# TensorE's queue written out by hand from the late features to the end of attention

## The chip, the cores and the metric

The kernel runs on one core of one Trainium2 chip. A time is the device time of one execution in microseconds (us). Three executions of the kernel before took 1167.98, 1169.8 and 1173.2 us; their median, 1169.8, is the time before. The names of the engines in the profile are PE (TensorE matmul), PEld (TensorE weight load), DVE (VectorE), ACT (ScalarE), POOL (GpSimd) and SP (SyncE, which issues most DMAs).

## The reference

One layer of a decoder on 1024 positions of width 1024, in float32. Three groups of heads read the same normed input, and one output projection mixes them. A gated MLP follows.

```python
h = rms_norm(x, norm1_g)
proj = h @ w_in            # q 512 | k 512 | v 512 | forget gates 8 | conv a 256, b 256 | pool 256
q, k = rms_norm per head of 64;  att = forgetting_attention(q, k, v, fg + b_f)
conv = conformer_conv(conv_in, ...)      # a*sigmoid(b), 31 causal taps, LayerNorm, silu, @ conv_pw
pool = multiscale_pool(pool_in, ...)     # means over 2/4/8/16 positions minus self, @ pool_w, scale
x = x + concat([att, conv, pool]) @ w_out
up = causal_depthwise_conv(rms_norm(x, norm2_g) @ w_up, ffn_dw_w)
x = x + (silu(gate) * val) @ w_down

# forgetting_attention, for a block of 128 queries and the keys up to its end (8 heads of 64):
s = q @ k.T * 64**-0.5 + cum[query] - cum[key]     # cum: running sum of log_sigmoid(fg)
p = softmax(where(key <= query, s, -1e30)); out = p @ v
```

## The kernel before

Every matmul is made of three: each operand is split into a rounded high half and a low half (`split`: ScalarE casts the high half, L48; VectorE, or GpSimd where it is named, subtracts for the low half, L49), and `mm3` adds high x high (L53), high x low (L54) and low x high (L55). A sum stays in one PSUM bank of 128 x 512 floats until an engine evacuates it.

The stages, in the program's order:

- Features. The convolution's a and b and the pool input are projected. The first two blocks go with the arriving weights; the others (the late features, from L341) follow one after the other, in the banks named `mm`, of which there are four.
- Values (`values_in`). Eight tiles of 128 positions, eight k each: first 256 columns (192 matmuls), then 256 columns and the 8 gate logits. ScalarE evacuates each tile into `v` (L424) and `fgt` (L426).
- The gates (`gate_cumsum`). VectorE and ScalarE turn the logits into log gates `fz` (L368 to L375), TensorE transposes them (L381), and their running sum goes to DRAM as `cumd`, from where each head's row comes back as `ck`.
- Q and K (`heads_in`). Q in tiles of 512 columns, two tiles at a time with k outside, then K in two calls of 256 columns. Each tile is squared (ScalarE), reduced (VectorE), turned into a scale (GpSimd), and scaled into `qk` (VectorE, L460), which frees the bank. The weights of Q's last four k are split in turn by VectorE and GpSimd, into `w` out of the raw buffers `wr`.
- Work at the side (`side_work`, a generator that is stepped between the tiles): 31 taps for each of two channel blocks and two halves of the positions (`taps`, VectorE, L268, 120 multiply-adds of 128 x 512 and 4 starts), the pool's running means and differences `d` with their split `dhl` and product (`pool_work`, products into the banks named `tp`, two of them), and the convolution's LayerNorm, silu and product (`conv_tail`: transposes, `s_` with its split, products, all in `tp` banks).
- `prep_pair`. For two heads, Q and K are transposed (L402) and split into `qT`, `kh`, `kl`, four pieces of four transposes per pair.
- Attention. A stage is one head and one group g of two query blocks, in the order g = 3, 0, 2, 1. `scores` issues the products (L534, with the causal mask added as a product, L537), VectorE adds the running gate and keeps the row minimum in one pass (L539), ScalarE takes the exponential (L543), VectorE the reciprocal of the sum (L545), GpSimd scales (L546). `values` transposes the probabilities `p` into a bank `t`, up to four blocks of 128 at a time (L558), splits the bank into `pt`, and multiplies with the head's `vhl` (L567 to L569); the output goes to `matt` (L574). Scores run three stages ahead (`LOOK`). Between stages, the parts of the output projection that need only convolution and pool (`mix_out`, banks `f`) and the next heads' `prep_pair` are put in.
- Behind it the attention part of the output projection (banks `c`), the MLP's up and down projections.

What sets the order: the queue of each engine is written by the framework's scheduler, which simulates the program and issues what it finds ready, by the program's order where several are. So the generators and the places of `step` are hints, and TensorE's queue interleaves single matmuls of different parts. Each engine then runs its queue strictly in order; a waiting instruction holds what stands behind it. An order written by hand (`tc.manual_schedule`) exists in before only for SP in the last stage.

## Time and profile before

| | |
|---|---|
| median of three runs | 1169.8 us |
| the profiled execution | 1172.92 us, its span 1170.7 us |
| TensorE / VectorE / ScalarE / GpSimd busy | 1099.4 / 896.1 / 534.4 / 342.3 us |
| late features end | 79.4 us |
| first score product, last value product | 254.4 us, 442.9 us |
| up projection | about 512 to 926 us |

A busy TensorE is a union of matmul intervals with modelled ends; what it works through is better read from the distance of starts. The profile's rows by window have, for each engine, its busy time and the number of instructions, then the granted TensorE clock (1.00 is full speed). Rows of a timeline begin with start and duration. Rows of groups have "count | busy time, mean ns of one | idle time ahead of them and its releaser". An arrow `a <- b` in the names reads: a is written from b.

### The profile page before, as it was taken

The page shows a single profiled execution, that of the slowest core. Times are in us where ns is not written, and L with a number is a line of the kernel's source. Part 1 is how long each engine was busy: PE and PEld are TensorE (multiplying, and loading weights), DVE is VectorE, ACT ScalarE, POOL GpSimd, SP SyncE. Part 2 cuts the span into 40 slices and gives each one's busy share as a digit, 9 for nine tenths or more (in the row PEclk, how much of TensorE's full clock was granted, in tenths as well). Part 3 has the DMA queues.
Part 4 walks back from the last instruction along what each step waited for, and adds up shares of the span by engine and source line. Part 5 has one row for each costly group of instructions (what it writes and reads, how often), then busy time and mean ns, then how long its engine had stood idle before and what let it go on. Part 6 is the DMA issues. An engine that isn't in the chain of part 4 may idle for free.

```text
span 1170.7 us, 14708 instructions
## 1 busy us (share of the span) xinstructions
PE 1099.4 (94%) x5476; PEld 912.8 (78%) x5476; DVE 896.1 (77%) x1262; ACT 534.4 (46%) x785; POOL 342.3 (29%) x335
## 2 busy tenths in 40 slices
PE   7995998899999989869999999999999999899987
PEld 6775977887888878758888888888888787688865
DVE  5899996468888665777887878788887655898673
ACT  7331322358878754445353535353544443243321
POOL 1480447557667742301212121212121210000010
PEclk9997999999999989969999999999999999899999
DMA  9130111033124131211212221212121497672362
GB/s 353 37 98 15 37 38 54 2 109 101 53 81 127 36 127 73 108 37 55 92 70 79 84 100 63 100 63 93 70 102 60 136 330 261 215 261 91 126 224 82
DMA packets 52792, 124.15 MB, mean 106 GB/s; under 512 B 6249, under 2 KB 11753, under 8 KB 49905
## 3 DMA queue, kind: packets, MB, share of 16 engines
q1 hardware_dynamic: 47056, 103.29, 26.4%
q0 software_dynamic: 5664, 19.93, 4.3%
q8 instruction: 43, 0.70, 0.2%
q14 instruction: 29, 0.23, 0.1%
HBM read 99.04 MB, written 19.96 MB: 102 GB/s over the span
## 4 chain that ended last, share of the span: by engine, by line
PE 58%; DVE 16%; issue 15%; DMA 5%; ACT 2%; POOL 2%; SPq 1%; POOLq 0%; DVEq 0%; ACTq 0%
PE b L55 12%; PE b L53 12%; PE b L54 12%; DVE acc L268 8%; PE s L534 2%; PE t L558 2%; DMA xr<-in_xT_dram 1%; PE f L53 1%; PE mm L53 1%; PE mm L54 1%; PE f L55 1%; PE c L53 1%; PE mm L55 1%; PE px L567 1%; PE f L54 1%
## 5 line engine op out<-in xcount | busy, mean ns | idle before, releaser
L865 POOL TENSOR_TENSOR ac<-ac 128x1024 f32<-128x1024 f32 x22 | 61.4, 2792 | 368.5 <-ACT u L846 266.5
L821 DVE SCALAR_TENSOR_TENSOR ac<-u,par,ac 128x1023 f32<-128x1023 f32 x88 | 112.6, 1280 | 8.9 <-ACT ac L819 7.9
L268 DVE SCALAR_TENSOR_TENSOR acc<-u,par,acc 128x512 f32<-128x512 f32 x120 | 105.9, 935 | 0.0
L53 PE MATMUL mm<-w,hh 128*128 128x256 f32 (+2 forms) x320 | 99.0, 311 | 3.8 <-DVE qk L460 3.8
L48 ACT CAST wsh<-ws 128x2048 fp32r<-128x2048 f32 x22 | 42.0, 1910 | 130.0 <-PE b L54 129.8
L54 PE MATMUL mm<-w,hh 128*128 128x256 f32 (+2 forms) x320 | 98.8, 310 | 0.0
L55 PE MATMUL mm<-w,hl 128*128 128x256 f32 (+2 forms) x320 | 98.8, 309 | 0.0
L49 DVE TENSOR_TENSOR dl<-dr,dh 128x1024 fp32r<-128x1024 f32 (+1 forms) x39 | 65.7, 1684 | 26.9 <-ACT dh L48 26.9
L546 POOL TENSOR_TENSOR p<-p,l 128x896 f32<-128x896 f32 (+3 forms) x64 | 72.7, 1150 | 32.0 <-DVE l L545 30.5
L48 ACT CAST dh<-dr 128x1024 fp32r<-128x1024 f32 (+1 forms) x39 | 54.6, 1401 | 58.5 <-PE y L55 24.6
L54 PE MATMUL x<-dl,dh 128*128 128x512 f32 x176 | 70.2, 399 | 4.8 <-DVE dl L49 4.8
L915 POOL DMA_DIRECT2D out_dram<-acc x16 | 8.7, 541 | 211.1 <-DVE acc L911 210.5
L55 PE MATMUL x<-dh,dl 128*128 128x512 f32 x176 | 69.8, 396 | 0.0
L53 PEld LDWEIGHTS mm<-w,hh 128*128 128x128 f32 x320 | 61.9, 193 | 7.4 <-issue 4.2
L819 ACT ACTIVATE ac<-u,par 128x1024 f32<-128x1024 f32 x44 | 50.7, 1152 | 31.2 <-DVE u L856 30.7
L54 PEld LDWEIGHTS mm<-w,hh 128*128 128x128 f32 x320 | 62.1, 194 | 3.3
L55 PEld LDWEIGHTS mm<-w,hl 128*128 128x128 f32 x320 | 62.2, 194 | 3.1
L48 ACT CAST dh<-res 128x1024 fp32r<-128x1024 f32 x22 | 23.1, 1052 | 87.6 <-PE y L55 63.4
L53 PE MATMUL x<-dh 128*128 128x512 f32 x176 | 54.9, 406 | 6.3 <-DVE acc L911 5.6
L49 DVE TENSOR_TENSOR wsl<-ws,wsh 128x2048 fp32r<-128x2048 f32 x22 | 50.4, 2290 | 12.8 <-ACT wsh L48 12.8
L49 DVE TENSOR_TENSOR pt<-t,pt 128x512 fp32r<-128x512 f32 (+1 forms) x80 | 49.5, 631 | 12.5 <-ACT pt L48 12.2
L714 DVE TENSOR_TENSOR ws<-wur 128x512 f32<-128x512 f32 x21 | 58.4, 2783 | 0.0
(316 smaller groups left out, 3327.3 us busy)
## 6 DMA issues: line engine op xcount, KB each, us to landing
wur<-in_w_up_dram SPq DMA_DIRECT2D x22, 1024.0 KB, 4.9
dr<-in_w_down_dram SPq DMA_DIRECT2D x66, 256.0 KB, 5.0
dr<-gd SPq DMA_DIRECT2D x55, 256.0 KB, 4.6
gd<-ac POOLq DMA_DIRECT2D x22, 512.0 KB, 3.0
wr<-in_w_in_dram SPq DMA_DIRECT2D x32, 256.0 KB, 2.7
res<-gd SPq DMA_DIRECT2D x22, 256.0 KB, 5.6
v<-in_x_dram SPq DMA_DIRECT2D x8, 512.0 KB, 8.9
ck<-cumd SPq DMA_DIRECT2D x8, 512.0 KB, 3.6
```

Source lines behind the costliest of these rows:

```text
L48: nc.scalar.copy(out=dst_hi, in_=src)
L49: (lo or nc.vector).tensor_tensor(out=dst_lo, in0=src, in1=dst_hi.bitcast(F32), op=ALU.subtract)
L53: nc.tensor.matmul(ps, a_hi, b_hi, start=first, stop=False, skip_group_check=more)
L54: nc.tensor.matmul(ps, a_hi, b_lo, start=False, stop=False, skip_group_check=more)
L55: nc.tensor.matmul(ps, a_lo, b_hi, start=False, stop=last, skip_group_check=more)
L268: nc.vector.scalar_tensor_tensor(out=a, in0=u[:, c, o + j:o + j + 512], scalar=pc(PC_DW + c * CW + j), in1=a, op0=ALU.mult, op1=ALU.add)
L534: nc.tensor.matmul(ps[:, 0:c1 - c0], qT[:, i * P:(i + 1) * P], part[:, c0:c1], start=b == 0, stop=b == 1 and c1 < n)
L546: nc.gpsimd.tensor_tensor(out=pt[:, 0:n], in0=pt[:, 0:n], in1=l[:, 1:2].broadcast_to([P, n]), op=ALU.mult)
L714: eng.tensor_tensor(out=out, in0=a, in1=b, op=ALU.subtract)
L819: nc.scalar.activation(out=ac, in_=us, func=AF.Copy, scale=pc(w0 + 2))
L821: nc.vector.scalar_tensor_tensor(out=ac[:, j:S], in0=us[:, 0:S - j], scalar=pc(w0 + 2 - j), in1=ac[:, j:S], op0=ALU.mult, op1=ALU.add)
L865: nc.gpsimd.tensor_tensor(out=a[:, 1], in0=a[:, 1], in1=a[:, 0], op=ALU.mult)
```

## The change

From the late features to the end of attention TensorE's queue is now the program's order (`manual_schedule` for PE). The other engines are still ordered by the scheduler, which simulates them against that queue. The program's order is rewritten with it:

- The work at the side is parted. VectorE's own work (`vector_work`: taps and pool sums, from which `d`) is still stepped between tiles; what TensorE takes part in (`side_work`: the pool product, now `pool_out`, and `conv_tail`) is put at fixed groups of Q's and K's matmuls: the gate transposes behind Q's k=6, pieces of `side_work` behind every second k from 9 on, in K behind every fifth, and the first `prep_pair` inside K's second call.
- `log_gates` is cut off from `gate_cumsum` and issued after the values.
- The raw weight buffer `wr` is half as wide; the pool `rp` has four buffers instead of three.
- Attention is 80 turns of one bank of transposes. In a round k: transposes of turn k, scores (12 steps per 10 turns, 10 steps ahead), a `prep_pair` piece in three windows of rounds (2 to 8, 22 to 28, 42 to 48, every second), a quarter of a `mix_out` tile (rounds 10 to 49 four times in five, from 52 in each, two at times), then the value products of turn k-2 (`LAG`).
- The banks `t` go from three to two, the banks `px` from one to two, `ms` from one buffer to two, and `ms` with its rows of x is prepared a tile ahead (`mix_prep`). `load_cum` is moved out of `prep_head`, two heads ahead. Of the value products of a turn, the low half for j0 now comes last.

The diff, cut to its core:

```diff
-    rp = pa2.enter_context(tc.tile_pool(name="rp", bufs=3, **right))
+    rp = pa2.enter_context(tc.tile_pool(name="rp", bufs=4, **right))
...
-            t = rp.tile([P, 1056], F32, name=name, bufs=2)
+            t = rp.tile([P, 528], F32, name=name, bufs=2)
...
+    def pool_out(i):
+        hl_ = []
+        for half in range(2):
+            dhl = sp.tile([P, 2, 512], F32R, name="dhl", tag="shl")
+            split(dhl[:, 0], dhl[:, 1], pool_d[i][:, half * 512:half * 512 + 512])
+            hl_.append(dhl)
+        yield
+        for half in range(2):
+            ps = tpps()
+            mm3(ps, pw_hl[:, 0, i, :], pw_hl[:, 1, i, :], hl_[half][:, 0], hl_[half][:, 1], True, True)
+            nc.vector.tensor_scalar(out=mcp[half][:, 2 + i, :], in0=ps, scalar1=pc(PC_PS + i), scalar2=None,
+                                    op0=ALU.mult)
+            yield
...
+    def vector_work():
+        yield from taps(0)
+        pool_consts()
+        yield from pool_sums(0)
+        yield from pool_sums(1)
+        yield from taps(1)
+
     def side_work():
-        yield from taps(0)
-        yield from pool_work()
-        yield from taps(1)
+        yield from pool_out(0)
+        yield from pool_out(1)
         yield from conv_tail(0)
         yield from conv_tail(1)
 
-    bg = side_work()
+    vw, sw = vector_work(), side_work()
...
+    ordered = ExitStack()
+    ordered.enter_context(tc.manual_schedule(engines={mybir.EngineType.PE}))
...
-            step(7)
+            step(6)
...
+                side(t0 // per * KT + k)
...
+    values_in(C_V, 256, 0, later(load_two, 4, C_V + 256, 264, nc.gpsimd), 2)
+    values_in(C_V + 256, 264, 1, later(load_wide, 4, 0, nc.gpsimd), 2)
     for k in range(4, KT):
         load_wide(0, k, (nc.vector, nc.gpsimd)[k % 2])
-    gate_cumsum()
-    heads_in(0, 0, 512, later(load_two, 4, 512, 256, None), 6)
-    for _ in bg:
+    log_gates()
+
+    def side_q(n):
+        step(1 if n < 19 else 9)
+        if n == 6:
+            gate_cumsum()
+        elif n >= 8 and n % 2:
+            next(sw, None)
+
+    heads_in(0, 0, 512, later(load_two, 4, 512, 256, None), side_q)
+    heads_in(512, 1, 256, later(load_two, 4, 768, 256, nc.gpsimd), lambda n: n % 5 == 4 and next(sw, None))
...
+    heads_in(768, 1, 256, [], lambda n: n in (4, 12, 20, 28) and next(pp, None))
...
-    psT = pb.enter_context(tc.tile_pool(name="psT", bufs=3, space=PSUM))
-    psX = pb.enter_context(tc.tile_pool(name="psX", bufs=1, space=PSUM))
+    psT = pb.enter_context(tc.tile_pool(name="psT", bufs=2, space=PSUM))
+    psX = pb.enter_context(tc.tile_pool(name="psX", bufs=2, space=PSUM))
...
+    def turn(h, g, jj):
         p0, p1 = pr_t[h, 2 * g], pr_t[h, 2 * g + 1]
-        po = xbank()
-        for jj in range(g + 1):
-            ps = psT.tile([P, 512], F32, name="t", tag="t")
-            j0, j1 = 2 * jj, 2 * jj + 1
-            srcs = [(p0, j0), (p1, j0), (p1, j1)] if jj == g else [(p0, j0), (p1, j0), (p0, j1), (p1, j1)]
-            for a, (p, j) in enumerate(srcs):
-                nc.tensor.transpose(out=ps[:, a * P:(a + 1) * P], in_=p[:, j * P:(j + 1) * P], identity=ident)
-            n = len(srcs) * P
-            pt = bp.tile([P, 2, 512], F32R, name="pt", bufs=4)
-            split(pt[:, 0, 0:n], pt[:, 1, 0:n], ps[:, 0:n])
-            c = 512 - n if jj == g else 0
-            for b in range(2):
-                if jj == 0 and b == 1:
-                    pt0 = pt
-                else:
-                    nc.tensor.matmul(po[:, 0:256], vhl[:, j0, :], pt[:, b, 0:256], start=jj + b == 0, stop=False)
-                nc.tensor.matmul(po[:, c:256], vhl[:, j1, :], pt[:, b, 256:n], start=False, stop=False)
-        nc.tensor.matmul(po[:, 0:256], vhl[:, 0, :], pt0[:, 1, 0:256], start=False, stop=True)
+        ps = psT.tile([P, 512], F32, name="t", tag="t")
+        j0, j1 = 2 * jj, 2 * jj + 1
+        srcs = [(p0, j0), (p1, j0), (p1, j1)] if jj == g else [(p0, j0), (p1, j0), (p0, j1), (p1, j1)]
+        for a, (p, j) in enumerate(srcs):
+            nc.tensor.transpose(out=ps[:, a * P:(a + 1) * P], in_=p[:, j * P:(j + 1) * P], identity=ident)
+        n = len(srcs) * P
+        pt = bp.tile([P, 2, 512], F32R, name="pt", bufs=4)
+        split(pt[:, 0, 0:n], pt[:, 1, 0:n], ps[:, 0:n])
+        return pt, n
+
+    def values(h, g, jj, pt, n, po):
+        vhl = hd[h]
+        c = 512 - n if jj == g else 0
+        j0, j1 = 2 * jj, 2 * jj + 1
+        nc.tensor.matmul(po[:, 0:256], vhl[:, j0, :], pt[:, 0, 0:256], start=jj == 0, stop=False)
+        for b in range(2):
+            nc.tensor.matmul(po[:, c:256], vhl[:, j1, :], pt[:, b, 256:n], start=False, stop=False)
+        nc.tensor.matmul(po[:, 0:256], vhl[:, j0, :], pt[:, 1, 0:256], start=False, stop=jj == g)
...
+            for n in range(4):
+                w = wo[4 + n, half]
+                mm3(ps, m[:, 0, n, :], m[:, 1, n, :], w[:, 0], w[:, 1], n == 0, n == 3)
+                if n == 1 and t % 4 < 3:
+                    nxt = mix_prep(t + 1, half)
+                if n == 3:
+                    nc.vector.tensor_tensor(out=x2_slice(t, half), in0=ps, in1=xr, op=ALU.add)
+                yield
...
+    stages = [(h, g) for h in range(H) for g in (3, 0, 2, 1)]
+    turns = [(n, jj) for n, (h, g) in enumerate(stages) for jj in range(g + 1)]
+
+    def all_scores():
+        for n, st in enumerate(stages):
+            for _ in scores(*st):
+                yield n
...
+    LAG = 2
+    sc = all_scores()
+    done = [sum(g + 1 for h, g in stages[:n]) for n in range(len(stages) + 1)]
     prep_head(0)
-    for st in stages[:LOOK]:
-        scores(*st)
-    pp = None
-    for n, (h, g) in enumerate(stages):
-        at = n // 4
-        if n % 4 == 0 and at + 1 < H:
-            prep_head(at + 1)
-        if n + LOOK < len(stages):
-            scores(*stages[n + LOOK])
-        if n % 8 == 1 and at + 2 < H:
-            pp = prep_pair(at // 2 + 1, fbank)
-        if pp is not None:
-            next(pp, None)
-            prep_done[0] |= at == 5 and n % 8 == 7
-        values(h, g)
-        if n >= 4 and (n % 2 == 0 or n > 28):
-            next(fill, None)
-    for _ in fill:
-        pass
+    load_cum(1, bp)
+    n_sc, last = 0, 0
+
+    def more_scores(upto, turned):
+        nonlocal n_sc, last
+        while n_sc < upto and last is not None:
+            nxt = n_sc // 12 * 4 + (0, 0, 0, 0, 1, 1, 2, 2, 2, 2, 3, 3)[n_sc % 12]
+            if nxt >= 4 and turned < done[nxt - 3]:
+                break
+            last = next(sc, None)
+            n_sc += 1
+
+    more_scores(10, 0)
+    pairs = {k: pr for pr, k0 in ((1, 2), (2, 22), (3, 42)) for k in range(k0, k0 + 8, 2)}
+    preps = {}
+    fill1, fill2 = mix_first(), mix_second()
+    banks, waiting = {}, []
+
+    def value(n, jj, pt, w):
+        h, g = stages[n]
+        if jj == 0:
+            banks[n] = xbank()
+        values(h, g, jj, pt, w, banks[n])
+
+    for k, (n, jj) in enumerate(turns):
+        h, g = stages[n]
+        if k % 10 == 2 and h + 1 < H:
+            prep_head(h + 1)
+        if k % 10 == 3 and h + 2 < H:
+            load_cum(h + 2, bp)
+        waiting.append((n, jj, *turn(h, g, jj)))
+        more_scores(10 + (12 * (k + 1)) // 10, k + 1)
+        if k in pairs:
+            if pairs[k] not in preps:
+                preps[pairs[k]] = prep_pair(pairs[k], fbank)
+            next(preps[pairs[k]])
+        if k >= 10 and k < 50:
+            run(fill1, (k % 5 != 0))
+        if k >= 52:
+            run(fill2, 1 + (k % 8 == 0))
+        if len(waiting) > LAG:
+            value(*waiting.pop(0))
+    run(fill1, 32)
+    while waiting:
+        value(*waiting.pop(0))
+        run(fill2)
+    run(fill2, 32)
```

How the queues move, at three places. The first is ScalarE's queue during the first values: `v_134` are evacuations of the first values' tiles, `dhl` the high halves of the pool difference. Before:

```order
L48 CAST w<-wr 128x2x264 x2
L424 ACTIVATE v_134<-mm,rstd 128x256 x5
L48 CAST dhl<-d 128x512 x2
L424 ACTIVATE v_134<-mm,rstd 128x256 x2
L48 CAST w<-wr 128x512 x2
```

With the change:

```order
L48 CAST w<-wr 128x2x264 x2
L446 ACTIVATE v_134<-mm,rstd 128x256 x4
L48 CAST dhl<-d 128x512 x2
L446 ACTIVATE v_134<-mm,rstd 128x256 x3
L48 CAST w<-wr 128x512 x2
```

The casts of `dhl` have moved ahead of the fifth evacuation.

The second is TensorE's queue around the gate transposes, during Q (`hh_118` is the eighth part of the normed input that belongs to k=4, and so on; 79 of Q's 192 matmuls stand ahead of the transposes). Before:

```order
L53 MATMUL mm<-w,hh_118 128x512
L54 MATMUL mm<-w,hh_118 128x512
L55 MATMUL mm<-w,hl_126 128x512
L53 MATMUL mm<-w,hh_119 128x512
L381 MATMUL tp<-ident,fz 8x128 x8
L54 MATMUL mm<-w,hh_119 128x512
L55 MATMUL mm<-w,hl_127 128x512
```

With the change:

```order
L53 MATMUL mm<-w,hh_120 128x512
L54 MATMUL mm<-w,hh_120 128x512
L55 MATMUL mm<-w,hl_128 128x512
L403 MATMUL tp<-ident,fz 8x128 x8
L53 MATMUL mm<-w,hh_121 128x512
L54 MATMUL mm<-w,hh_121 128x512
L55 MATMUL mm<-w,hl_129 128x512
```

Now 42 of Q's matmuls stand ahead of them, those of k=0 to k=6 of the first two tiles.

The third is TensorE's queue in attention: `t` transposes, `s` scores, `px` value products, `f` the fill. Before, near the start:

```order
L568 MATMUL px<-pt,vhl 128x256
L558 MATMUL t<-ident,p_2506 128x128
L534 MATMUL s<-kh,qT 128x512
L534 MATMUL s<-kl,qT 128x512
L567 MATMUL px<-pt,vhl 128x256
L568 MATMUL px<-pt,vhl 128x128
L558 MATMUL t<-ident,p_2521 128x128
L558 MATMUL t<-ident,p_2506 128x128
```

With the change, one round in the second half:

```order
L585 MATMUL t<-ident,p_4371 128x128
L585 MATMUL t<-ident,p_4403 128x128
L561 MATMUL s<-kh,qT 128x128
L561 MATMUL s<-kl,qT 128x128
L564 LDWEIGHTS ident_b
L564 MATMUL s<-mask_b,ident_b 128x128
L53 MATMUL f<-wo,ms 128x512
L54 MATMUL f<-wo,ms 128x512
L55 MATMUL f<-wo,ms 128x512
L595 MATMUL px<-pt,vhl 128x256
L597 MATMUL px<-pt,vhl 128x256 x2
L598 MATMUL px<-pt,vhl 128x256
```

Single transposes and products were interleaved; now transposes, scores, fill and value products of a round each stand together.

More of the change, by code (lines that the diff above doesn't have):

```diff
@@ L299, in conv_tail @@
             yield
+        yield
         for n in range(2):
@@ L430, in values_in, with heads_in @@
                     m()
-    def heads_in(c0, src, w, then, steps):
+    def heads_in(c0, src, w, then, side):
         chunks = range(2) if w == 512 else (c0 // 256 % 2,)
@@ L523, in scores @@
         qT, kh, kl = qkT[h]
-        vhl, ck = hd[h]
+        ck = cks[h]
         for i in (2 * g, 2 * g + 1):
@@ new lines, in scores @@
+                if c1 == n:
+                    l = bp.tile([P, 2], F32, name="l", bufs=8)
+                    nc.scalar.activation(out=pt[:, 0:n], in_=pt[:, 0:n], func=AF.Exp, scale=-1.0, bias=init,
+                                         accum_out=l[:, 0:1])
+                    nc.vector.reciprocal(out=l[:, 1:2], in_=l[:, 0:1])
+                    nc.gpsimd.tensor_tensor(out=pt[:, 0:n], in0=pt[:, 0:n], in1=l[:, 1:2].broadcast_to([P, n]),
+                                            op=ALU.mult)
+                    pr_t[h, i] = pt
@@ L621, in mix_work, with mix_second @@
         yield from mix_out(1, 0)
-        while not prep_done[0]:
-            yield
+    def mix_second():
         load_wo(1, 4, bp)
@@ L652, in tile_hybrid_block, with run @@
-    for _ in fill:
-        pass
+    def run(it, n=1):
+        for _ in range(n):
+            next(it, None)
+    LAG = 2
+    sc = all_scores()
+    done = [sum(g + 1 for h, g in stages[:n]) for n in range(len(stages) + 1)]
+    prep_head(0)
+    load_cum(1, bp)
[8 more added lines that the diff above has]
+            n_sc += 1
```

114 lines of the change are left out of this document (46 added, 68 removed).

## The prediction

> **What bounds the kernel now.** I read the page first, then the busy time of each engine stage by stage, then TensorE's waits, then single rows.
>
> ```profile
> span 1170.7 us, 14708 instructions
> PE 1099.4 (94%) x5476; PEld 912.8 (78%) x5476; DVE 896.1 (77%) x1262; ACT 534.4 (46%) x785; POOL 342.3 (29%) x335
> ```
>
> TensorE is busy for 94% of the span. An order can only win the rest, stretches at half clock, and the gaps that modelled ends hide. The stages that the change reorders lie between 79.4 (late features done) and 443.2 us (last value product):
>
> ```profile
> core 0: us, PE busy (x) PEld busy (x) DVE busy (x) ACT busy (x) POOL busy (x), PEclk, DMA share, GB/s
> 79.40:159.10 79.70, 66.59 (x464) 62.83 (x463) 79.63 (x111) 21.05 (x45) 22.78 (x11) 0.91 0.15 41
> 159.10:254.40 95.30, 88.33 (x591) 80.44 (x590) 60.31 (x123) 27.70 (x47) 58.75 (x88) 0.98 0.13 33
> 254.40:268.70 14.30, 11.02 (x48) 6.96 (x47) 10.37 (x36) 12.38 (x25) 13.16 (x14) 0.77 0.46 139
> 300.00:420.00 120.00, 118.03 (x773) 99.08 (x772) 99.46 (x291) 97.13 (x212) 84.14 (x72) 1.00 0.27 83
> 420.00:437.50 17.50, 12.50 (x74) 11.28 (x72) 8.91 (x18) 9.18 (x19) 5.29 (x5) 0.80 0.32 115
> 512.00:926.00 414.00, 413.82 (x1784) 337.03 (x1785) 330.47 (x276) 186.22 (x193) 68.59 (x40) 0.99 0.22 79
> ```
>
> Three things stand here. From 79.4 to 159.1 VectorE has no gap (79.63 of 79.70), so it sets the pace there, not TensorE. In attention's middle TensorE is busy for 118 of 120 us, with VectorE at 83% and ScalarE at 81%. Attention's two ends are thin: 11.0 of 14.3 us and 12.5 of 17.5, both at a reduced clock. The up projection gives the pitch of a 512-column matmul, 414.00/1784 = 0.232 us. For 256 columns it is 10.00/88 = 0.114 us:
>
> ```profile
> 84.00:94.00 10.00, 10.00 (x88) 10.00 (x87) 0.00 (x0) 2.25 (x5) 1.00 0.28 78
> ```
>
> TensorE's waits between 40 and 440 us, the longest ones:
>
> ```profile
> PE tp L53 <- ACT dhl L48: 13.1, 1, 13.1
> PE t L558 <- DVE pt L49: 4.6, 2, 3.7
> PE mm L53 <- DVE qk L460: 3.8, 2, 3.4
> PE tp L53 <- ACT s__1624 L48: 3.0, 1, 3.0
> ```
>
> The largest is the pool projection, which stands in TensorE's queue in front of value matmuls that were ready.
>
> **Part 1, the projections.** The change takes the pool projection out of the value matmuls, but three VectorE results still gate TensorE. These are their rows, in VectorE's and ScalarE's timelines:
>
> ```profile
> L268 DVE SCALAR_TENSOR_TENSOR acc<-u,par,acc x120: 715/739/1829, 45.4 to 184.3; 128x512 f32<-128x512 f32 x120
> 109.03 0.16 DVE L248 COPY d<-m 128x16 f32<-128x16 f32 x1
> 145.53 0.68 DVE L49 TENSOR_TENSOR w<-wr,w 128x512 fp32r<-128x512 f32 x1
> 150.61 0.68 DVE L49 TENSOR_TENSOR w<-wr,w 128x512 fp32r<-128x512 f32 x1
> 156.48 2.73 DVE L268 SCALAR_TENSOR_TENSOR acc<-u,par,acc 128x512 f32<-128x512 f32 x4
> 159.14 0.21 DVE L375 SCALAR_TENSOR_TENSOR fz<-fgt,fz 128x64 f32<-128x64 f32 x1
> 109.22 1.14 ACT L48 CAST dhl<-d 128x512 fp32r<-128x512 f32 x2 [15.30 <-DVE d L248]
> 110.27 0.47 ACT L424 ACTIVATE v<-mm,rstd 128x256 f32<-128x256 f32 x1
> ```
>
> A tap of the depthwise convolution (L268) follows the next by 2.73/4 = 0.68 us. In the new VectorE order three more taps stand ahead of d, so d comes at 109.2 + 3 x 0.68 = 111.2. ScalarE casts d between the fourth and the fifth evacuation of the first values, and the four mm banks are then full: the second values' first tile needs the fifth evacuation, at 111.2 + 1.14 + 0.47 = 112.8. TensorE has finished the first values' 192 matmuls at 79.4 + 192 x 0.114 = 101.3. So a wait of about 11.5 us replaces the one of 13.1; the place is another, the size nearly the same.
>
> What a long wait leaves behind is seen in two windows, and in the wait that lies in the second of them:
>
> ```profile
> 102.00:115.50 13.50, 5.61 (x24) 5.41 (x25) 13.47 (x24) 1.80 (x4) 0.00 (x0) 0.50 0.01 1
> 200.00:210.00 10.00, 6.76 (x41) 6.46 (x42) 3.69 (x9) 5.21 (x8) 8.10 (x11) 0.83 0.11 28
> 208.71 0.73 PE L53 MATMUL tp<-s__1624,cw_hl 128*128 128x512 f32 x2 [2.96 <-ACT s__1624 L48]
> ```
>
> After the long wait the matmuls run at a granted clock of 0.50 until 115.5, so 5.6 us of work takes twice its time and 2.8 us are lost. After the 3.4 us wait near 200, the mean of 0.83 says that (1 - 0.83) x 10/0.5 = 3.4 us were at half clock, a loss of 1.7; the 3.0 us wait at 208.7 lies in the same window and adds nothing to it. [...]
>
> The second values end at 112.8 + 192 x 0.118 (264 columns, scaled from 0.114) + 2.8 = 138.3, and Q's first four k at 138.3 + 24 x 0.232 = 143.9. Then k=4 needs its low half from VectorE. Eight taps more, two dhl and four pool scalings fewer stand ahead of it (these six at about 0.65): 145.5 + 0.6 + 8 x 0.68 - 6 x 0.65 = 147.6. In the same way k=6 comes at 152.7. The log gates have five taps more and the same six fewer: 159.3 + 3.4 - 3.9 = 158.8. TensorE has done Q up to k=6 by 152.7 + 6 x 0.232 = 154.1 and stands before the gate transposes until 158.8. In the old order those transposes came with 79 Q matmuls done, in the new with 42: the work that covered VectorE's lateness is now behind it.
>
> What is left then: 150 x 0.232 (Q) = 34.8, 384 x 0.114 (K) = 43.8, 36 x 0.232 (pool and convolution products) = 8.4, and 56 transposes x 0.11 = 6.2; the sum is 93.2. To this come 2.8 for half clock after the gates' wait of 4.7 and 5 for new stalls. I take 5 from two kinds of row: the convolution's tail waited 3.0, an evacuation 3.4, and both chains are still there, now in fixed slots. First score at 158.8 + 93.2 + 2.8 + 5 = 259.8 against 254.4: **+5.4** (from -2.4, no loss beyond the 252.0, to +10, twice the new stalls).
>
> **Part 2, attention.** Groups between 256 and 437 us, by form:
>
> ```profile
> L49 DVE TENSOR_TENSOR pt<-t,pt 128x512 fp32r<-128x512 f32 x48 | 32.5, 685 | 7.7 <-ACT pt L48 7.4
> L539 DVE CUSTOM_DVE_ANT_0 p<-s,ck 128x512 f32<-128x512 f32 x39 | 26.6, 682 | 2.2 <-PE t L558 0.9 <-PE s L537 0.5 <-POOL p L546 0.3
> L48 ACT CAST pt<-t 128x512 fp32r<-128x512 f32 x48 | 27.8, 588 | 6.4 <-PE px L568 4.2 <-PE t L558 1.0 <-DVE matt L574 0.5
> L558 PE MATMUL t<-ident,p 128*128 128x128 f32 x288 | 45.0, 281 | 4.8 <-DVE pt L49 4.6
> L53 PE MATMUL f<-wo,ms 128*128 128x512 f32 x64 | 26.5, 414 | 0.3
> ```
>
> By pitch, TensorE's attention work is 336 transposes x 0.11 = 37 (pitch below), 192 f products x 0.232 = 44.5, and scores, masks and value products of 73,728 + 8,192 + 73,728 columns (counted from the loops) at 0.232/512 us = 70.5: 152 us. Its first and last product:
>
> ```profile
> 254.42 0.39 PE L534 MATMUL s<-kh,qT 128*128 128x512 f32 x1
> 442.92 0.33 PE L569 MATMUL px<-pt,vhl 128*128 128x256 f32 x1
> ```
>
> The stage took 443.2 - 254.4 = 188.8, less 20 of the next stage's 512-column products (4.6) that ran inside it: 184.2. So 32 us are lost. By the windows some 10 go before 300 us and 9 in the tail after 420, and 12 in the middle's 120. Of the middle's, part is the price of changing over:
>
> ```profile
> 343.18 0.48 PE L534 MATMUL s<-kh,qT 128*128 128x512 f32 x1
> 343.50 0.40 PE L534 MATMUL s<-kl,qT 128*128 128x512 f32 x1
> 343.73 0.93 PE L558 MATMUL t<-ident,p 128*128 128x128 f32 x7
> 344.42 0.31 PE L534 MATMUL s<-kh,qT 128*128 128x128 f32 x1
> ```
>
> Seven transposes take 0.69, about 0.1 each (0.11 with a record missing here and there, which I use). The first product after transposes has 0.32 instead of 0.232 to itself before the next one starts. 0.09 x about 72 changes from transposes to products is 6 us. The new order has 80 turns and 12 groups of prep transposes, so 8.
>
> The start of the new order: ten score steps, then the first turn. Its way is in these rows:
>
> ```profile
> 255.10 0.68 DVE L539 CUSTOM_DVE_ANT_0 p<-s,ck 128x512 f32<-128x512 f32 x1
> 268.68 0.57 PE L558 MATMUL t<-ident,p 128*128 128x128 f32 x2
> L543 ACT ACTIVATE p<-p,m 128x1024 f32<-128x1024 f32 x8 | 9.2, 1154 | 2.0 <-DVE m L539 1.9
> L546 POOL TENSOR_TENSOR p<-p,l 128x1024 f32<-128x1024 f32 x8 | 15.2, 1898 | 5.8 <-DVE l L545 5.8
> ```
>
> In VectorE's new order the last evacuations of K stand ahead of the first reduce (3.4 us after the first score, now 0.7). Four reduces (2.9), exponential (1.15), reciprocal (0.16), scaling (1.9) and 2 for hand-overs make 11.5, against 14.3 before. With 3.7 us of scores done, 7.8 are lost. In rounds 0 to 9 VectorE has more than TensorE: 12 reduces 7.7, 8 reciprocals 1.2, 10 low halves 6.4, 4 outputs 1.6, 8 prep pieces 6.0, together 22 against 15 us, so 7 lost: 14.8 by then, against 10 before. Rounds 10 to 79: changes of form 7, the two other prep windows 3, waits of 2 to 8 (the middle of before had 12 less 4 to 5 for changes of form), of which I take 3 because a quarter of a fill tile stands behind most turns, and a tail of 2, since the last turns follow with fill between them. All in all 14.8 + 7 + 3 + 3 + 2 = 29.8 us are lost instead of 32. I take **-2.5** (from -15, the start as before and no wait in the rounds, to +12.5, late rounds below). Behind attention nothing is moved.
>
> Sum: +5.4 - 2.5 = +2.9. On the profiled execution (1172.92, span 1170.7) that is 1176; its time is 3.1 above the median of the three runs, so against 1169.8 it is **1173**.
>
> **Rivals.** *Attention gains in full.* For it: the thin ends (3.3 and 5.0 us idle, clock 0.77 and 0.80), and the wait of 3.7 in the tail. If prep is spread well and the rounds keep TensorE fed, the loss is 10 + 6 (changes of form) + 2 (tail) = 18 instead of 32, -14, and with stalls hidden in the projections (+1) the time is 1157. Against it: the middle is 118 of 120 busy already.
>
> *Rounds that are late* (slower). Place: every turn. Two banks of transposes instead of three, and values two turns behind: a turn's bank is freed after transposes 0.44, cast 0.59 and low half 0.69, 1.7 us plus hand-overs and whatever is queued ahead on VectorE and ScalarE, which are at 83% and 81%. A round is 152/80 = 1.9 us, so a bank is asked again after 3.8. It decides once more than 2.1 us are queued ahead (three reduces of 0.68); a quarter of a microsecond in 60 of 80 rounds is 15 us more than I put in: +12.5 in attention, 1188. [...]
>
> *The order is nearly the old one.* The engines that pace a stage are not reordered by hand, and give the same time: 1170. For it: 79.63 of 79.70. Against: 37 Q matmuls moved behind the gates.
>
> **How the numbers follow.** Three runs of before spread over 0.4%, so a change under 0.5% (5.85 us) can't be told from none. Forecast 1173 (1164 to 1180): 0.40, of it 0.27 within 0.5% and 0.13 slower. Full gain, 1157: 0.32, faster. Late rounds, 1188: 0.20, slower. Nothing moves, 1170: 0.08. So faster 0.32, same 0.35, slower 0.33. The range 1153 to 1189 takes in most of both sides.
>
> **What would show it.** In the new trace: a wait of 10 to 12 us at the second values' first tile, gate transposes at 158 to 160, first score at 257 to 263. VectorE without a gap before 159. First turn 10 to 13 us after the first score; last value product 178 to 185 after it. If the gates' transposes come by 150, or the mm wait is under 5 us, part 1 is wrong; if TensorE's waits for pt or t exceed 12 us in attention, the late rounds are right; if the last product comes within 172 us, the full gain.

## The result, and the profile after

The changed kernel takes 1183.34 us (median of four runs, 1181.6 to 1185.25) against 1170.38 us for the kernel before beside it. The ratio is 1.011 with a 95% interval of 1.0082 to 1.0139: slower by 13.0 us. That is inside the stated range and on the slower side of the forecast of 1173. The profiled execution took 1184.0 us. Two single executions among the experiments were disturbed (1814 us in e3, and 3393 us in e5, the one that was traced there) and are left out of the times below.

The page of the changed kernel, span and busy times:

```profile
span 1182.2 us, 14804 instructions
PE 1104.5 (93%) x5476; PEld 914.4 (77%) x5476; DVE 901.4 (76%) x1262; ACT 536.0 (45%) x785; POOL 353.3 (30%) x335
```

The number of matmuls and their work are the same, so the 11.5 us that the span gained are waiting and a lower granted clock (mean 0.968 over the span, before 0.972). Where they arise is seen from the starts of the stages in the two traces (us):

| | before | after |
|---|---|---|
| first matmul of the first values | 79.2 | 88.4 |
| first of the second values | 118.5 | 111.8 |
| first of Q | 143.6 | 135.1 |
| gate transposes | 162.0 | 162.7 |
| first score | 254.4 | 263.8 |
| first transpose of attention | 268.7 | 275.8 |
| last value product | 442.9 | 450.3 |
| last product of attention's output projection (banks `c`) | 488.8 | 502.7 |
| last of the up projection | 935.3 | 948.0 |
| end | 1170.7 | 1182.2 |

So 9.4 us are lost by the first score. Another 4.5 are lost in attention: the stage from first score to the last `c` product lasts 238.9 us instead of 234.4. The rest of the kernel gives 2.4 back. The last `c` product is the fair mark, because before had 20 of the `c` products inside attention.

TensorE's busy time and clock by window (the columns as in the prediction):

```profile
core 0: us, PE busy (x) PEld busy (x) DVE busy (x) ACT busy (x) POOL busy (x), PEclk, DMA share, GB/s
40.00:79.40 39.40, 33.19 (x133) 25.69 (x132) 39.29 (x43) 10.29 (x19) 25.50 (x17) 0.91 0.20 56
79.40:159.10 79.70, 68.54 (x466) 61.98 (x464) 75.29 (x100) 19.64 (x43) 38.58 (x14) 0.93 0.13 37
263.80:300.00 36.20, 28.13 (x160) 22.46 (x159) 27.67 (x83) 28.86 (x59) 26.46 (x25) 0.81 0.30 88
300.00:420.00 120.00, 114.31 (x745) 97.75 (x744) 98.28 (x275) 92.63 (x200) 75.29 (x65) 0.99 0.26 78
420.00:437.50 17.50, 17.50 (x116) 15.49 (x115) 13.13 (x41) 14.82 (x33) 16.01 (x14) 1.00 0.39 123
```

Two things stand out against before. VectorE, which had no gap from 79.4 to 159.1, now has one of 4.4 us there. And GpSimd is busy for 38.6 us instead of 22.8 in the same window, in 14 instructions against 11. Attention's thin tail has become full, 17.50 of 17.50 us where it was 12.50; its middle has become thinner, 114.3 of 120 where it was 118.0.

TensorE's waits between 40 and 470 us in the changed kernel, the longest ten:

```profile
PE mm L54 <- DVE w L49: 7.0, 1, 7.0
PE mm L55 <- POOL w L49: 5.7, 2, 4.5
PE s L561 <- DVE m L566: 5.1, 6, 3.2
PE t L585 <- DVE pt L49: 4.1, 5, 1.1
PE f L53 <- DVE qT L432: 4.0, 2, 2.0
PE tp L403 <- DVE fz L395: 3.6, 1, 3.6
PE mm L53 <- ACT w L48: 2.2, 2, 1.7
PE tp L302 <- DVE y L295: 2.1, 2, 1.2
PE mm L54 <- POOL w L49: 1.6, 1, 1.6
PE c L53 <- DVE matt L605: 1.6, 1, 1.6
```

The wait of 13.1 us for the pool projection is gone. In its place stand waits for Q's weights (from VectorE 7.0, from GpSimd 1.6, from the cast 1.7), for the late features' weights from GpSimd (4.5), and for the log gates (3.6). Single rows of GpSimd, VectorE, ScalarE, SyncE and TensorE show how those of Q hang together (the first of SyncE is from the table of its waits):

```profile
134.63 18.02 POOL L49 TENSOR_TENSOR w<-wr,w 128x512 fp32r<-128x512 f32 x1 [12.96 <-ACT w L48]
133.49 13.98 DVE L277 SCALAR_TENSOR_TENSOR acc<-u,par,acc 128x512 f32<-128x512 f32 x21
147.40 0.67 DVE L49 TENSOR_TENSOR w<-wr,w 128x512 fp32r<-128x512 f32 x1
150.13 1.39 DVE L277 SCALAR_TENSOR_TENSOR acc<-u,par,acc 128x512 f32<-128x512 f32 x2
SPq L138 <- POOL w L49: 28.4, 1, 28.4
152.68 0.80 SPq L138 DMA_DIRECT2D wr<-in_w_in_dram  x2
155.84 0.69 DVE L49 TENSOR_TENSOR w<-wr,w 128x512 fp32r<-128x512 f32 x1 [4.32 <-ACT w L48]
155.19 1.37 ACT L48 CAST w<-wr 128x512 fp32r<-128x512 f32 x2 [19.21 <-DMA wr<-in_w_in_dram]
162.70 1.66 PE L403 MATMUL tp<-ident,fz 128*8 128x128 f32 x7 [3.61 <-DVE fz L395]
```

GpSimd's low half for k=5 begins at 134.63 and lasts 18.02 us. It ends at 152.65, 1.1 us after VectorE ran out of work (150.13 + 1.39 = 151.5). Only then is a raw buffer free: SyncE's queue stands 28.4 us until this instruction releases it, and the transfers for k=6 and k=7 go out from 152.68. So the cast for k=6 comes at 155.19, VectorE stands for 4.32 us, and everything behind it in VectorE's queue, the log gates included, comes some 4 us late. In the kernel before the same instruction took 4.26:

```profile
143.10 4.26 POOL L49 TENSOR_TENSOR w<-wr,w 128x512 fp32r<-128x512 f32 x1 [15.22 <-ACT w L48]
```

### The profile page after: what moved, and what is told of

Its sections match the earlier page's. It is cut to its first block, busy times and chain, and to the rows that moved or that the text cites. A ratio compares the mean times of both kernels' runs of the same rounds, so it can differ in the third digit from the quotient of the medians.

```text
span 1182.2 us, 14804 instructions
## 1 busy us (share of the span) xinstructions
PE 1104.5 (93%) x5476; PEld 914.4 (77%) x5476; DVE 901.4 (76%) x1262; ACT 536.0 (45%) x785; POOL 353.3 (30%) x335
## 4 chain that ended last, share of the span: by engine, by line
PE 66%; issue 15%; DVE 6%; DMA 5%; POOL 4%; ACT 3%; SPq 0%; POOLq 0%; ACTq 0%; DVEq 0%
PE b L53 12%; PE b L55 12%; PE b L54 12%; PE mm L55 4%; PE mm L53 4%; PE mm L54 4%; PE t L585 2%; POOL w L49 2%; PE s L561 2%; PE c L53 1%; PE f L53 1%; PE c L54 1%; PE c L55 1%; DMA wr<-in_w_in_dram 1%; PE px L597 1%
## 5 line engine op out<-in xcount | busy, mean ns | idle before, releaser
L49 POOL TENSOR_TENSOR w<-wr,w 128x512 fp32r<-128x512 f32 (+1 forms) x22 | 52.2, 2382 | 41.3 <-ACT w L48 41.2
```

Of the source, the lines that this page charges most:

```text
L49: (lo or nc.vector).tensor_tensor(out=dst_lo, in0=src, in1=dst_hi.bitcast(F32), op=ALU.subtract)
```

## The experiments

Theory P: the projections carry most of the loss, through VectorE's queue and what hangs on it (Q's low halves, the log gates). Rival A: attention's rounds carry it. The kernel before was timed beside each group; ratios are to it.

**Each half alone.** The kernel was cut at the start of attention (before `mxb` is opened) and the halves of the two kernels were joined. First, projections as before, attention as in the change:

```diff
     pa.close()
+    ordered = ExitStack()
+    ordered.enter_context(tc.manual_schedule(engines={mybir.EngineType.PE}))
...
-    psT = pb.enter_context(tc.tile_pool(name="psT", bufs=3, space=PSUM))
-    psX = pb.enter_context(tc.tile_pool(name="psX", bufs=1, space=PSUM))
+    psT = pb.enter_context(tc.tile_pool(name="psT", bufs=2, space=PSUM))
+    psX = pb.enter_context(tc.tile_pool(name="psX", bufs=2, space=PSUM))
...
```

From there on every line of attention is the changed kernel's.

> The projections word for word as before, in the scheduler's order; attention as in the change (turns, rounds, two banks of transposes and two of values, TensorE by hand). Theory P (the projections carry most): first score at 254 to 256 us, 185 to 187 us to the last value product, and 2 more to the next stage, 3 us more than before: 1173 to 1176. Rival A (attention carries most): 1179 or more. Rival N (attention's order is worth nothing either way): 1170 to 1172.

Measured 1174.35 us, ratio 1.0025 (1.0014 to 1.0036), 3.1 us above before. The first score came at 256.8 us, 2.4 later than in the trace before. Up to there the traces have the same instructions in the same order on TensorE, VectorE, ScalarE, GpSimd and SyncE, so these 2.4 us lie between two executions and not between two queues. A difference of this size in one stage of single traces need not come from an edit. From first score to the last `c` product 236.7 us passed, 2.3 more than before; behind it 679.4 us, 2.5 less. TensorE's waits in attention here:

```profile
PE s L535 <- DVE m L540: 6.9, 8, 3.2
PE f L53 <- DVE qT L410: 4.0, 2, 2.0
PE t L559 <- DVE l L547: 1.8, 1, 1.8
PE c L53 <- DVE matt L579: 1.6, 1, 1.6
PE t L559 <- DVE pt L49: 0.8, 2, 0.4
```

Then the other half: projections as in the change, the hand order closed in front of attention, attention as before.

```diff
     heads_in(768, 1, 256, [], lambda n: n in (4, 12, 20, 28) and next(pp, None))
     pa.close()
+    ordered.close()
...
-    psT = pb.enter_context(tc.tile_pool(name="psT", bufs=2, space=PSUM))
-    psX = pb.enter_context(tc.tile_pool(name="psX", bufs=2, space=PSUM))
+    psT = pb.enter_context(tc.tile_pool(name="psT", bufs=3, space=PSUM))
+    psX = pb.enter_context(tc.tile_pool(name="psX", bufs=1, space=PSUM))
...
```

> The other half: projections as in the change with TensorE by hand, attention word for word as before, in the scheduler's order. Theory P: first score at 262 to 265 us, attention 184 us, the time 9 us above before: 1179 to 1182. Rival A: 1173 or less. If both halves together are not the change's 11 to 13 us, the rest lies in how the one hands over to the other.

Measured 1178.65 us, ratio 1.0058 (1.0038 to 1.0077), 7.4 us above before, just below what was expected. First score at 263.4, from there to the last `c` product 233.6 us. The two halves together, 3.1 + 7.4 = 10.5 us, agree with the change's 13.0 within their intervals; the 2.5 us between them are not assigned. So theory P holds by size: some 7 to 9 us are the projections', 2 to 4 are attention's, and none of attention's forecast gain is there. Some of attention's loss may come back later: behind the last `c` product 681.9 us passed before and 681.6 here, but 677.7 to 681.1 in the eleven traces with the rewritten attention. Whether that is the text or spread is not shown.

**The hand order alone, on the new text.** First, the hand order in attention only, with the scheduler ordering the rewritten projections.

```diff
-    ordered = ExitStack()
-    ordered.enter_context(tc.manual_schedule(engines={mybir.EngineType.PE}))
     for f in late:
...
     pa.close()
+    ordered = ExitStack()
+    ordered.enter_context(tc.manual_schedule(engines={mybir.EngineType.PE}))
```

> TensorE in program order in attention alone; up to there the scheduler orders it again, from the changed program text. Theory P (two thirds of the loss arises in the projections: first score at 263.8 us instead of 254.4): first score at 254 to 258 us, attention as in the change (187 us from first score to last value product), time 1172 to 1176. Rival A (the rounds of attention are what costs): 1180 or more. If the scheduler makes something else of the new text, the first score says so.

Measured 1182.59 us, ratio 1.0097 (1.0067 to 1.0126). The first score came at 261.5, not at 254 to 258, so theory P's expectation was wrong, and the time is the one that rival A asked for. It doesn't speak for rival A, because 7.1 us were lost before the hand order began: the scheduler makes something nearly as slow of the new text. GpSimd's low halves of Q took 10.29 and 9.90 us here:

```profile
136.16 10.29 POOL L49 TENSOR_TENSOR w<-wr,w 128x512 fp32r<-128x512 f32 x1 [11.39 <-ACT w L48]
150.60 9.90 POOL L49 TENSOR_TENSOR w<-wr,w 128x512 fp32r<-128x512 f32 x1 [4.15 <-ACT w L48]
```

So it isn't TensorE's strict order by itself that costs; the rewritten text, with the pool product out of the values, has the same weakness in either order.

Second, the hand order in the projections only, with the scheduler ordering the rewritten attention (`ordered.close()` moved to the end of K).

> TensorE in program order up to the end of K's projection alone; in attention the scheduler orders it, from the changed text (two transpose banks, two value banks, turns). Theory P: first score still at 262 to 265 us, time 1178 to 1182. Rival A: the loss goes with attention's order, time 1170 to 1174.

Measured 1183.91 us, ratio 1.0107 (1.0084 to 1.0131): 1.9 us above what was expected. First score 263.9; from there to the last `c` product 239.0 us, as in the change. The rewritten attention costs the same whether its order is written by hand or by the scheduler, and the old text (233.6 and 234.4 us) is the faster one.

**The late features.** The hand order begins behind them.

```diff
-    ordered = ExitStack()
-    ordered.enter_context(tc.manual_schedule(engines={mybir.EngineType.PE}))
     for f in late:
...
             step(6)
+    ordered = ExitStack()
+    ordered.enter_context(tc.manual_schedule(engines={mybir.EngineType.PE}))
```

> The hand order begins behind the late features instead of ahead of them. In the change the first values' matmuls began at 88.4 us, before at 79.2. Theory P (VectorE and GpSimd pace this stage up to the log gates, so that delay is absorbed): first values at 79 to 81 us, but gate transposes still at 160 to 164 us and the time within 3 us of the change, 1180 to 1185. Rival L (the 9 us of delay reach the end): gate transposes by 156 us, time 1174 to 1178.

Measured 1183.72 us, ratio 1.0097 (1.0064 to 1.0129). The first values now began at 79.0 us, 9.4 earlier than in the change, and the first score came at 263.5, against 263.8. So almost nothing of the delay of the late features reaches the first score, as expected. What absorbs it are two rows, a wait of TensorE at the second values' first tile and GpSimd's low half for k=7:

```profile
109.94 0.59 PE L53 MATMUL mm<-w,hh 128*128 128x264 f32 x1 [8.34 <-ACT v L446]
150.11 13.03 POOL L49 TENSOR_TENSOR w<-wr,w 128x512 fp32r<-128x512 f32 x1 [4.20 <-ACT w L48]
```

The first is the bank that the casts of the pool difference hold up. The gate transposes came at 156.9, 5.8 earlier than in the change and outside the expected 160 to 164, but k=7's weight then came at 163.2, and the gain was gone.

**Q's low halves on VectorE alone.**

```diff
-        load_wide(0, k, (nc.vector, nc.gpsimd)[k % 2])
+        load_wide(0, k, nc.vector)
```

> The low halves of Q's weights for k=5 and k=7 are made by VectorE instead of GpSimd. In the change GpSimd's half for k=5 lasted 18.0 us (134.6 to 152.7) while VectorE ran its taps back to back, and the weights of k=6 waited for its raw buffer. Theory G (GpSimd was kept out): k=5 ready at 149 to 150 us, no 4.3 us wait of VectorE for the cast of k=6, gate transposes at 158 to 160 instead of 162.7, time 1178 to 1181. Rival (VectorE's queue is simply that long): two more halves on VectorE, gate transposes at 163 to 165, time 1183 to 1186.

Measured 1180.18 us, ratio 1.0067 (1.0046 to 1.0089). In the trace the waits for k=5 to 7 are gone, two long ones are left:

```profile
148.34 0.80 PE L54 MATMUL mm<-w,hh 128*128 128x512 f32 x1 [7.05 <-DVE w L49]
158.61 1.87 PE L403 MATMUL tp<-ident,fz 128*8 128x128 f32 x8 [3.52 <-DVE fz L395]
```

Gate transposes at 158.6 and first score at 259.8. With two more instructions on the fuller engine the gates come 4.1 us earlier, so it was GpSimd's part in them that had come late, and the rival falls. The gain in time, 3.2 us between medians, is in the expected range.

**VectorE as the pace.** Every second tap of the second channel block is left out, so that part of the convolution is missing from the output.

```diff
-                nc.vector.scalar_tensor_tensor(out=a, in0=u[:, c, o + j:o + j + 512], ...)
+                if c == 0 or j % 2:
+                    nc.vector.scalar_tensor_tensor(out=a, in0=u[:, c, o + j:o + j + 512], ...)
```

> The change, but every second tap of the convolution's second channel block is left out (30 of 120 multiply-adds, 0.68 us each, about 16 us of it ahead of the log gates); that part of the computation is missing. Theory V (VectorE paces all up to the gates): gate transposes at 145 to 150 us instead of 162.7, first score at 246 to 252, time 1164 to 1171. Rival T (TensorE's order itself, or GpSimd and the weights' transfers): gate transposes at 156 or later, time 1177 or more.

Measured 1170.63 us, ratio 0.9993 (0.9977 to 1.0009): 12.7 us less than the change for 30 x 0.68 = 20 us less work on VectorE. First score 253.0, 10.8 earlier. The time is at the upper end of what was expected. The gate transposes (154.5) missed the expected 145 to 150, and the first score missed 246 to 252 by 1 us. Why is in one row:

```profile
147.84 0.80 PE L54 MATMUL mm<-w,hh 128*128 128x512 f32 x1 [6.28 <-DVE w L49]
```

k=4's low half came as late as ever: 93 taps (the 4 starts counted in) stand ahead of it in VectorE's queue here and 96 in the change, because the scheduler puts others forward when some are left out. VectorE is the pace up to the gates, but what TensorE needs of it stands at a place that the scheduler's simulation chooses.

**The gates later.** As e4, and the gate transposes behind Q's group 14.

```diff
-        if n == 6:
+        if n == 14:
             gate_cumsum()
```

> As e4 (Q's low halves for k=4 to 7 on VectorE), and the gate transposes behind Q's group 14 instead of 6, so that 90 instead of 42 of Q's matmuls stand ahead of them. Theory C (the transposes were put ahead of the work that covered VectorE's lateness): the wait of 3.9 us before them and the half clock behind it go, first score at 254 to 256 us instead of 259.8, time 1174 to 1177. Rival (the same VectorE results are needed next, so another wait takes its place): first score within 1.5 us of 259.8, time 1178 to 1181.

Measured 1177.65 us, ratio 1.0053 (1.0033 to 1.0073), 2.5 us less than e4, between the two expectations and not clear of e4 by the intervals. For its stages the next kernel stands in, which is the same up to the end of K: there the first score came at 259.3, 0.5 earlier than in e4. By that trace the rival is right: the transposes now come at 168.1 and the wait ahead of them is gone, but TensorE stands 3.2 us in the middle of them, for a scaling of the pool product on VectorE. So the work that was moved behind the gates explains little of the loss.

**The fill off the prep rounds.** As e5, and in attention:

```diff
-            run(fill1, (k % 5 != 0))
+            run(fill1, k not in pairs)
```

> As e5, and in attention's rounds 10 to 49 the fill leaves out the eight rounds with a piece of prep instead of every fifth round. In the change TensorE waited twice for 2.0 us (2.27 between starts) before the fill, for VectorE's qT of the prep piece. Theory F (the wait is the fill's for its bank): both waits go, 4 us less than e5, time 1170 to 1173. Rival V (VectorE is the pace of the prep windows): the waits turn up at other products, time within 1.5 us of e5.

Measured 1181.88 us, ratio 1.0089 (1.0057 to 1.0121): not 4 us less than e5 but 4.2 more, so both expectations missed the time. The waits moved, as rival V said, from the fill to the transposes of the prep pieces, which ask for the same two banks `f`, and they grew:

```profile
PE f L424 <- DVE qT L432: 4.8, 3, 1.7
PE f L424 <- DVE kl L432: 2.1, 2, 1.3
```

6.9 us instead of 4.0. The price at these places is that of two banks between fill and prep, and both VectorE's split and the banks take part in it.

**Late features free, low halves on VectorE, gates later.** The hand order begins as in e3, and one step of the side work is taken per tile of values:

```diff
-    values_in(C_V, 256, 0, later(load_two, 4, C_V + 256, 264, nc.gpsimd), 2)
-    values_in(C_V + 256, 264, 1, later(load_wide, 4, 0, nc.gpsimd), 2)
+    values_in(C_V, 256, 0, later(load_two, 4, C_V + 256, 264, nc.gpsimd), 1)
+    values_in(C_V + 256, 264, 1, later(load_wide, 4, 0, nc.gpsimd), 1)
-        load_wide(0, k, (nc.vector, nc.gpsimd)[k % 2])
+        load_wide(0, k, nc.vector)
-        if n == 6:
+        if n == 14:
```

> As e5 (Q's low halves on VectorE, gate transposes behind group 14), and the hand order begins behind the late features as in e3; steps of VectorE's side work one per tile of values. Theory V: the taps ahead of k=4's low half are 90 instead of 96 and the first values begin at 79 us, low half of k=4 at 143 to 145, first score at 255 to 257, time 1173 to 1177. Rival L (the late features are what is lost): first score at 251 or earlier.

Measured 1176.4 us, ratio 1.0035 (1.0022 to 1.0049), the best version of the changed kernel, and still 4.5 us above before. First score 258.3, later than the expected 255 to 257, though k=4's low half came when it was expected (144.7). Its longest wait is the one that the prediction had named:

```profile
PE mm L53 <- ACT v L446: 8.4, 1, 8.4
PE mm L54 <- DVE w L49: 4.5, 3, 3.1
```

The steps of the side work, one or two per tile, left VectorE's queue without a change: e3 (two steps) and this run (one) have the same 47 multiply-adds ahead of the first d, 86 ahead of k=4's low half and 101 ahead of the log gates. The likely reason is that the scheduler takes a tap whenever nothing else is ready in its simulation.

**VectorE by hand too**, with the low halves and the gates ahead of more taps.

```diff
-    ordered.enter_context(tc.manual_schedule(engines={mybir.EngineType.PE}))
+    ordered.enter_context(tc.manual_schedule(engines={mybir.EngineType.PE, mybir.EngineType.DVE}))
...
     pa.close()
+    ordered.close()
+    ordered = ExitStack()
+    ordered.enter_context(tc.manual_schedule(engines={mybir.EngineType.PE}))
...
-        load_wide(0, k, (nc.vector, nc.gpsimd)[k % 2])
+        load_wide(0, k, nc.vector)
+        step(5 * (k == 5))
...
-        step(1 if n < 19 else 9)
+        step(2 if n < 19 else 9)
```

Three steps are taken per tile of values instead of two, and three inside `log_gates`.

> VectorE too is held to the program's order up to the end of K (attention as in the change), with Q's low halves on VectorE and the taps spread so that 88 to 93 instead of 96 to 103 stand ahead of them, and 96 instead of 108 ahead of the log gates; three taps per tile of values, two per group of Q. Theory V (VectorE's place for the low halves and the gates is what holds TensorE): low half of k=4 by 142 us, gate transposes by 150, first score at 248 to 254, time 1168 to 1173. Rival (the same VectorE work has to be done by then, so the waits move to the convolution's tail or to the evacuations): first score at 257 or later, time 1176 or more.

Measured 1235.87 us, ratio 1.0541 (1.0522 to 1.0561). First score 303.7. Neither expectation saw this size. In program order VectorE's queue stands at each tile of Q and K for GpSimd's scale, as its own waits between 40 and 320 us show, and TensorE's wait for k=4's low half grew to 14.7; another of 15.1 is for the low half of the pool difference (`dhl`):

```profile
DVE qk L484 <- POOL ss L482: 52.9, 23, 5.6
```

```profile
PE mm L54 <- DVE w L49: 17.8, 3, 14.7
```

A better place of the low halves on VectorE was therefore not tested cleanly: the taps that were to stand behind them had been stepped ahead, and the evacuations had no work between them.

**Rounds that are late.** Value products three turns behind instead of two.

```diff
-    LAG = 2
+    LAG = 3
```

> The change with the value products three turns behind their transposes instead of two. Rival R of the prediction (every round waits for its split): TensorE has a round more of cover, attention shorter by 5 us or more, time 1174 to 1178. Theory (the rounds past 300 us wait for little; the loss is at the start and at the prep windows): within 2 us of the change, 1181 to 1186.

Measured 1182.53 us, ratio 1.0103 (1.007 to 1.0136), within a microsecond of the change. From first score to the last `c` product it took 236.5 us. That is 2.4 less than in the change, but the attention of the change took 236.1 to 239.1 in seven traces of kernels that share it (e9 left out). The waits of transposes for a split went from 4.1 to 2.6 us, all of it small:

```profile
PE s L561 <- DVE m L566: 4.8, 3, 3.2
PE f L53 <- DVE qT L432: 3.4, 2, 1.7
PE t L585 <- DVE pt L49: 2.6, 3, 1.4
```

A round more of cover for the value products wins nothing that the timing shows. The edit leaves the two banks of transposes as they are; the rival of late rounds falls by both, this run and the 4.1 us that the transposes wait in the change.

## Why the prediction was right or wrong

**The time.** 1183.3 lies in the range of 1153 to 1189, but that range took in nearly every rival, so there is little merit in it. It lies 3 us above the likeliest case's own 1164 to 1180, and the loss of 13.0 us is four times the 3.2 that were forecast. The likeliest case read the signs of the two parts as plus and minus, and they were both plus.

Of the signs that the prediction named, one held: the first turn 12.0 us after the first score. The others missed: gate transposes at 162.7 (158 to 160), first score at 263.8 (257 to 263), a gap in VectorE before 159 where none was to be, the last value product 186.5 us after the first score (178 to 185), and a wait of 0.8 us at the second values' first tile instead of 10 to 12. By its own words (under 5 us) this short wait makes part 1 wrong as a chain of events; what of it stood is told next.

**Part 1, +5.4 forecast, +9.4 measured.** Step by step: the pool difference d was forecast for 111.2, and came at 110.2; the second values' first tile at 112.8, and came at 111.8; k=4's low half ready at 147.6, and came at 148.0. These steps, counted from VectorE's queue and one pitch per tap, held to a microsecond. From the gate transposes to the first score 101.0 us were forecast (93.2 of work, 2.8 of half clock, 5 of stalls), and 101.1 passed. In part that is luck: behind 172 us TensorE stood for 3.6 us (91.79 less 88.22 busy), not 5, so the work must have been some 1.4 longer. The 2.8 of half clock was an estimate, taken over from the loss behind the wait of 13.1 in the trace before. It held for the gates: behind their wait of 3.61 the granted clock was 0.50 until 168.0 and 0.69 in the mean from 162.7 to 172.0, a loss of (1 - 0.69) x 9.3 = 2.9.

The step that failed is "In the same way k=6 comes at 152.7". It counted VectorE's instructions and left out that the raw buffer of k=6 had to wait for GpSimd's low half of k=5, which was put at nothing. That half took 18.0 us, k=6's cast came at 155.2, its low half at 156.5 (155.84 + 0.69), and the gates at 162.7 instead of 158.8. The miss of 4 us is this term. With GpSimd taken out (e4) the trace shows 158.6 and 259.8, where the prediction had 158.8 and 259.8. So close an agreement is luck too, since e4 has two more low halves on VectorE (1.2 us) and not the wait of 11.5.

A second error cost little. The prediction let the reordered stages begin at 79.4, but the hand order begins ahead of the late features, where GpSimd's low halves of their weights hold TensorE's queue (4.5 us), with a granted clock of 0.91 from 40 to 79.4 us where before had 1.00; the first values began 9.2 us late. So the wait of 11.5 us at the second values' first tile was not there (1.05 between starts): TensorE reached it late. With the late features left to the scheduler it is there, 8.3 us in e3 and 8.4 in e10. Either way that bank opens at 110 to 112. Of the 2.8 us of half clock that were put behind this wait the change shows none: the granted clock was 1.00 from 111.8 to 135.1. In e3 the first products behind it start 0.22 us apart, in the change 0.12. In e3 the gates came 5.8 us earlier, and GpSimd's low half for k=7 (13.0 us) took it back, first score 263.5. With GpSimd out, the first score came at 258.3 with the late features free (e10) and at 259.3 with them in the hand order (e6): about 1 us.

**Part 2, -2.5 forecast, +2 to +4.5 measured.** The first turn was forecast 11.5 us after the first score, and came 12.0 after it; the wait of 3.2 us for the first reduce behind K's last evacuations was in that term. The thin tail was won back, as the row of 420 to 437.5 shows, and from 300 to 420 us the granted clock was 0.99 (before 1.00). What failed is the size of three terms of the sum:

- Up to 300 us (about twelve rounds) 16.8 us were lost, 36.2 less the work by pitch, where 14.8 were forecast. Of these 2.0 us 0.9 are a slip: the five terms of rounds 0 to 9 add up to 22.9 and not to 22, so the prediction's own figures give 15.7, and about -1.6 for the part. The granted clock of 0.81 up to 300 us has no term in the sum.
- From 300 us to the last value product 17.7 were lost, 150.3 less the work by pitch, where 15 were. The two prep windows were put at 3 together; the fill waits 2.0 us each for its bank there, and the granted clock was 0.87 behind the first of these waits (336 to 348 us).
- Behind the last value product 1.95 pass before the next product, in `c`, where none were forecast, because before had run `c` products between the last value products.

That these three are what attention costs is read from the waits; the one edit that tried one of them, e6, made it worse.

**The rivals.** Full gain: wrong, attention lost (e11, 1.0025). Late rounds: the slower side was right but not its mechanism (TensorE's waits for pt in attention are 4.1 us, where it asked for more than 12, and e8 wins nothing). Nothing moves: wrong by the interval.

**What stays open.** Whether the old attention text wins by its shorter turns of transposes, its third `t` bank, or its `c` products in the tail is not separated: e2 and e12 show only that the text and not the order decides (239.0 against 233.6 us). In the projections GpSimd's low half accounts for 4 us of the 9.4; that the rest comes from VectorE's queue is borne out by e7, which takes 20 us of work off it, but no edit of its order alone was clean (e9). And no version tried that does the whole computation beats the kernel before.

## What to carry to other kernels

An engine put in program order needs its inputs in that order too. Here TensorE's side was rewritten while the engine that paces the stage kept a queue laid out by a simulation. Before such a change, list for each operand of the hand-ordered queue which engine makes it, what stands ahead of it there, and who must free its buffer; the operand made by an engine off the path (here GpSimd) is the one that is missed. Time the rewritten text under the old scheduler too: here it lost nearly as much in either order (e1, e2), so the hand order itself was not what cost. And compare stages by one mark that both kernels pass with the same work done, not by the end of a stage into which the next has been drawn.

## What the runs showed of the hardware

The same subtraction of 128 x 512 on GpSimd, for Q's weights, took 4.26 us before, 18.02 in the change, 10.29 and 9.90 in e1, 11.01 and 13.03 in e3. The rows of VectorE beside them (in e1 and e3 from 143 us on) have no gap; in the change, and for the second one of e1 and of e3, VectorE stopped 1.1 us before the end. In e7 the first one took 10.69 and the second 1.28:

```profile
151.90 1.28 POOL L49 TENSOR_TENSOR w<-wr,w 128x512 fp32r<-128x512 f32 x1 [6.05 <-ACT w L48]
```

While the one of 18.02 us lasted in the change, VectorE began some 26 instructions, most of them taps. In the kernel before the taps have a median of 0.74 us and a longest of 1.83. Two rows there overlap, GpSimd's beginning 0.14 us ahead, and the tap takes 1.79 us, 1.05 above the median:

```profile
151.74 1.39 POOL L49 TENSOR_TENSOR w<-wr,w 128x512 fp32r<-128x512 f32 x1 [4.38 <-ACT w L48]
151.88 1.79 DVE L268 SCALAR_TENSOR_TENSOR acc<-u,par,acc 128x512 f32<-128x512 f32 x1
```

What made these instructions long is not shown: the rows give their lengths and what ran beside them, and e4 gives the gates 4.1 us earlier with Q's low halves off GpSimd.
